# The last output chunk in written order: weights split once, the first token half normalized among the second half's products

## The chip, the cores and the metric

The kernel runs on one core of one Trainium2 chip. The metric is the device time of one launch in microseconds (us), the median of three runs. Beside the runs stands one profiled execution with its trace; rows are quoted with times from the start of its span. The engines are TensorE (PE in the rows; PEld is its weight load), VectorE (DVE), ScalarE (ACT), GpSimd (POOL) and the queue that issues most transfers (SP).

## The reference

One layer of a diffusion backbone over 512 latent tokens and 256 context tokens, model width 2048: a modulated RMSNorm, two attention mixers in parallel (differential attention and multi-head latent attention), an output projection, a second modulated RMSNorm, and a gated channel mixer of width 5632 whose gate passes a convolution of width 3 over the tokens. What matters here is its end:

```python
def _conv_ffn(h, w_up, conv_w, conv_b, w_down):
    g, u = jnp.split(h @ w_up, 2, axis=-1)
    gp = jnp.pad(g, ((0, 0), (pad, pad), (0, 0)))
    g = sum(gp[:, j:j + T] * conv_w[j] for j in range(CONV_W)) + conv_b
    return (jax.nn.silu(g) * u) @ w_down
...
x = x + g2 * _conv_ffn(h2, w_up[l], conv_w[l], conv_b[l], w_down[l])
return _rmsnorm(x, final_w)
```

The final norm divides each token by its root mean square over all 2048 features, so no output of a token can be scaled before the last of its features is known.

## The kernel before

Activations lie with features on the 128 partitions and the 512 tokens along the free axis, so one tile of 128 features is 128 x 512. Every product is made from float32 operands split in two parts: a high part cast to the matmul's format (`sc.copy` on ACT, tile `wh` or `ah`) and the rest (`ve.tensor_tensor` subtract on DVE, tile `wl` or `al`). `mm3` (L104 to L106) makes one product from three matmuls: high by high, high by low, low by high.

The channel mixer has 44 feature tiles (`ft`). From the fourth on, the up projection is a list of jobs in a manual schedule: PE, ACT, DVE and SP keep the order in which the program writes their instructions. A tile `ft` takes seven jobs `("p", ft, k)`, k from 0 to 6, of 8 + 8 matmuls (L981 with 512 columns, L983 with 256). Job i runs on PE (`run`), while `cast(i + 2)` and `low(i + 2)` split the weights two jobs ahead and `act_after` and `vec_after` handle the results of job i - 1. Two rings of three buffers load the raw weights: `ra` (tile `wr`) and `rb` (tile `rb`); `used` counts the uses of a buffer, and when it is free, `pump` issues the next load on SP. The down projection sums 11 chunks of four feature tiles; chunks 0 to 9 run as jobs `("d", c, dp)` among the up jobs, and their results are added in DRAM (`x1_d`, an accumulating transfer that POOL issues, L1002).

After job `("p", 43, 6)` four steps give the last activation: the gate is put together (L1024, L1025), scaled and convolved (`gate_in` L805, `convolve` L810 and L812), passed through SiLU (L817), multiplied (L821) and split (`ah` L823, `al` L827). The last chunk of the down projection needs it as its fourth feature tile. It stands behind the manual schedule and is ordered by the planner: `down` is called once for tokens 0 to 255 and once for tokens 256 to 511. Each call goes through 8 blocks of weights (`dp`), loads each block (L90, 512 KB), splits it whole (L80, L81), and for each of its two output tiles `dt` makes 4 products (12 matmuls of 256 columns) in a PSUM bank of its own and adds them to the residual:

```python
ve.scalar_tensor_tensor(out=x[:, ts], in0=po, scalar=modx[:, 80 + dt:81 + dt],
                        in1=x[:, ts], op0=ALU.mult, op1=ALU.add)
then(dt)
```

The first call also loads the residual tiles (L838, 16 of 256 KB). `then` squares tiles 0 to 11 (ACT, L673) and sums the squares on POOL (L674). When both calls are done, the Ln and Exp tables are loaded, and for each half `token_norm` sums over the partitions with matmuls against ones (L680, L684, the last four tiles each with a matmul of its own), makes the inverse root (`rstd`, L159 to L164), and 16 times scales a tile (DVE, L1085) and stores 128 KB (SP, L1086).

Of the kernel before, what the change touches and what calls it, by code (L numbers as in the profile page):

```python
# [17 lines left out]
P = 128  # L18
D = 2048
# [33 lines left out]
def layer_kernel(ctx: ExitStack, tc: tile.TileContext, small, rope, c_row, cc_row, x_t, ctx_t, ada, ada_k,  # L53
# [11 lines left out]
    def nm(s):  # L65
        n[0] += 1
        return f"{s}{n[0]}"
# [589 lines left out]
    ap_ = tc.alloc_tile_pool(name="ap2", bufs=32, side="right", reuse_waits="tile")  # L657
# [5 lines left out]
    for h in range(16):  # L663
        hl = a2k(F32R), a2k(F32R)
        split(hl[0], hl[1], oraw[h])
        osp.append(hl)
# [76 lines left out]
    def normed(kt):  # L743
# [4 lines left out]
        hx[kt] = (a2k(F32R), a2k(F32R) if kt >= 8 else hp.tile([P, T], F32R, tag="h12", name=nm("h12"), bufs=8))  # L748
# [7 lines left out]
    def sums(j):  # L756
# [4 lines left out]
        def put_away(t, src):  # L761
            t[j] = a2k(F32R) if t is t1 else spare.pop(0) if spare else b2k(F32R)
            split(*half(t[j]), src)
# [66 lines left out]
    def down(c, acts, ts, dst, then):  # L830

        for dp in range(8):
            wh, wl = wblock(w_dn[c, dp])
            for i in range(2):
                dt = dp * 2 + i
                x = dst[dt]
                if ts.start == 0:
                    nc.sync.dma_start(x, x1_d[dt])  # L838
                po = b_tile()[:, :ts.stop - ts.start]
                for f in range(FC):  # L840
                    o = f * 256 + i * P
                    mm3(po, (wh[:, o:o + P], wl[:, o:o + P]), [a[:, ts] for a in acts[f]], f == 0, f == FC - 1)
                ve.scalar_tensor_tensor(out=x[:, ts], in0=po, scalar=modx[:, 80 + dt:81 + dt],
                                        in1=x[:, ts], op0=ALU.mult, op1=ALU.add)
                then(dt)

# [52 lines left out]
    with tc.manual_schedule(engines={mybir.EngineType.PE, mybir.EngineType.Activation, mybir.EngineType.DVE,  # L899
# [47 lines left out]
        def cast(i):  # L947
            if i < last:
# [5 lines left out]
        def low(i):  # L954
            if i < last:
# [91 lines left out]
        for i, job in enumerate(jobs):  # L1047
            run(i)
            if job[0] == "p":
# [121 lines left out]
```

## Time and profile before

| what | us |
|---|---|
| median of the three runs | 2463.34 (2463.28 to 2465.94) |
| span of the profiled execution | 2463.1 |
| TensorE busy in it | 2379.3 (97%) |
| ends of the last up job's matmuls | about 2386.8 |
| first and last matmul of the last down chunk | 2380.61 and 2438.41 |
| first and last scaled output tile | 2443.22 and 2458.01 |

A row of the timeline gives the start, the duration (of a merged group, from its first start to its last end), engine, line, operation, output and inputs by the program's names, shapes and a count; in square brackets stands the idle time before it and what ended it. Matmuls are pipelined, so their durations overlap; the pace is read from the distance of the starts. A window row gives, for each engine, the busy time and in brackets the instructions, then the granted TensorE clock (1.00 is full speed), the mean share in which the DMA engines were busy, and GB/s. A group row gives the busy time in all and the mean duration in ns, then the idle time before.

### The profile page before, as it was taken

To read this page: it belongs to the slowest core of one execution; us is meant where nothing else is said; L and a number is where in the kernel's file an instruction comes from. 1 tells how busy PE (TensorE), PEld (TensorE's weight loads), DVE (VectorE), ACT (ScalarE), POOL (GpSimd) and SP (SyncE) were. 2 spreads that over 40 slices of the span, in tenths; PEclk is the share of its full clock that TensorE was granted. 3 is DMA by queue.
4 is the path that set the end of the run, shared out by engine and by line. 5 is a ranking of instruction groups with operands and counts; after the bars stand their busy time and mean duration, and the time that the engine had idled before them with its cause. 6 is when DMAs were issued, how large, how long until landed. Compare 5 with 4: busy or idle time off the path is not lost.

```text
span 2463.1 us, 33002 instructions
## 1 busy us (share of the span) xinstructions
PE 2379.3 (97%) x12796; PEld 1992.2 (81%) x12796; DVE 1728.2 (70%) x2274; ACT 1107.0 (45%) x1668; POOL 242.0 (10%) x266
## 2 busy tenths in 40 slices
PE   7999999999999999999999999999999999999996
PEld 3778888777677778888888888888888888888886
DVE  4668886398968777287676767676767675757576
ACT  4343121165645542254444445454545454545443
POOL 0000000121200002100101010101010101010113
PEclk8999999999999999999999999999999999999998
DMA  7868889554311158423656565656565555555564
GB/s 274 280 229 304 326 332 320 191 160 130 123 58 43 44 193 324 145 82 103 155 121 154 124 153 125 151 128 149 127 147 129 145 131 143 132 142 136 139 181 145
DMA packets 131859, 407.51 MB, mean 165 GB/s; under 512 B 14451, under 2 KB 25203, under 8 KB 123251
## 3 DMA queue, kind: packets, MB, share of 16 engines
q1 hardware_dynamic: 106422, 356.11, 43.9%
q0 software_dynamic: 25280, 49.30, 11.5%
q8 instruction: 100, 1.64, 0.3%
q14 instruction: 57, 0.47, 0.1%
HBM read 335.88 MB, written 69.48 MB: 165 GB/s over the span
## 4 chain that ended last, share of the span: by engine, by line
PE 84%; DVE 8%; ACT 3%; DMA 1%; issue 1%; POOL 1%; SPq 0%; DVEq 0%; ACTq 0%; POOLq 0%
PE y L981 11%; PE b L104 10%; PE b L105 10%; PE b L106 10%; PE z L981 6%; PE y L983 6%; PE s L104 4%; PE s L105 3%; PE s L106 3%; PE z L983 3%; PE s L482 3%; PE x L981 2%; PE pt L494 1%; PE x L983 1%; PE f L104 1%
## 5 line engine op out<-in xcount | busy, mean ns | idle before, releaser
L104 PE MATMUL b<-ah,wh 128*128 128x512 f32 (+1 forms) x768 | 287.2, 375 | 3.8 <-ACT ah L823 3.5
L105 PE MATMUL b<-al,wh 128*128 128x512 f32 (+1 forms) x768 | 287.2, 374 | 0.0
L106 PE MATMUL b<-ah,wl 128*128 128x512 f32 (+1 forms) x768 | 285.9, 373 | 0.0
L1002 POOL DMA_DIRECT2D x_d<-xs x160 | 139.7, 1007 | 1168.0 <-ACT xs L1001 1165.9
L80 ACT CAST wh<-wr 128x1024 fp32r<-128x1024 f32 (+2 forms) x134 | 132.4, 989 | 266.5 <-PE b L106 85.4
L957 DVE TENSOR_TENSOR wl<-wr,wh 128x1024 fp32r<-128x1024 f32 x125 | 152.5, 1220 | 129.2 <-ACT wh L951 129.2
L957 DVE TENSOR_TENSOR wl<-rb,wh 128x1024 fp32r<-128x1024 f32 x123 | 149.8, 1219 | 127.1 <-ACT wh L951 127.1
L81 DVE TENSOR_TENSOR wl<-wr,wh 128x1024 fp32r<-128x1024 f32 (+2 forms) x134 | 156.2, 1166 | 104.5 <-ACT wh L80 100.8
L951 ACT CAST wh<-wr 128x1024 fp32r<-128x1024 f32 x125 | 131.2, 1049 | 206.9 <-PE b L105 100.7
L951 ACT CAST wh<-rb 128x1024 fp32r<-128x1024 f32 x123 | 129.1, 1051 | 187.8 <-PE b L105 112.5
L957 DVE TENSOR_TENSOR wl<-ws,wh 128x1024 fp32r<-128x1024 f32 x123 | 150.0, 1220 | 88.9 <-ACT wh L951 88.9
L951 ACT CAST wh<-ws 128x1024 fp32r<-128x1024 f32 x123 | 128.2, 1042 | 138.3 <-DVE ws L925 52.8
L171 DVE CUSTOM_DVE_ANT_0 ada<-ada,cb,smt 128x2048 f32<-128x2048 f32 x64 | 151.1, 2363 | 54.7 <-DMA ada<-in_ada 54.6
L104 PEld LDWEIGHTS b<-ah,wh 128*128 128x128 f32 x768 | 145.8, 190 | 27.1 <-ACT ah L823 3.7
L106 PEld LDWEIGHTS b<-ah,wl 128*128 128x128 f32 x768 | 145.7, 190 | 25.6
L981 PE MATMUL y<-a2k,wh 128*128 128x512 f32 x656 | 164.0, 392 | 0.0
L105 PEld LDWEIGHTS b<-al,wh 128*128 128x128 f32 x768 | 146.1, 190 | 22.0
L104 PE MATMUL b<-a2k,wh 128*128 128x512 f32 (+1 forms) x376 | 139.8, 374 | 6.6 <-ACT a2k L751 5.0
L105 PE MATMUL b<-a2k,wh 128*128 128x512 f32 (+1 forms) x376 | 140.4, 374 | 0.4 <-DVE a2k L752 0.4
L106 PE MATMUL b<-a2k,wl 128*128 128x512 f32 (+1 forms) x376 | 139.2, 370 | 0.0
L981 PEld LDWEIGHTS y<-a2k,wh 128*128 128x128 f32 x656 | 118.6, 189 | 21.6
L981 PE MATMUL y<-b2k,wh 128*128 128x512 f32 x410 | 106.9, 391 | 0.0
(368 smaller groups left out, 5608.7 us busy)
## 6 DMA issues: line engine op xcount, KB each, us to landing
ada<-in_ada SPq DMA_DIRECT2D x64, 1024.0 KB, 6.0
rb<-in_w_up SPq DMA_DIRECT2D x123, 512.0 KB, 4.4
wr<-in_w_dn SPq DMA_DIRECT2D x96, 512.0 KB, 4.2
x_d<-xs POOLq DMA_DIRECT2D x160, 256.0 KB, 6.0
wr<-in_w_up SPq DMA_DIRECT2D x53, 512.0 KB, 4.3
wr<-in_w_f SPq DMA_DIRECT2D x34, 512.0 KB, 6.2
adak<-in_ada_k SPq DMA_DIRECT2D x32, 512.0 KB, 5.6
ada<-in_ada SPq DMA_DIRECT2D x32, 512.0 KB, 6.3
```

What stands on the lines that cost most here:

```text
L80: sc.copy(dst_h, src)
L81: ve.tensor_tensor(dst_l, src, dst_h.bitcast(F32), op=ALU.subtract)
L104: pe.matmul(out, st[0], mv[0], start=start, stop=False, **kw)
L105: pe.matmul(out, st[0], mv[1], start=False, stop=False, **kw)
L106: pe.matmul(out, st[1], mv[0], start=False, stop=stop, **kw)
L171: ve.tensor_tensor_reduce(out=junk, in0=w, in1=vec, op0=ALU.mult, op1=ALU.add, scale=1.0, scalar=col("b_ada", j), accum_out=dst[:, j:j + 1])
L482: pe.matmul(s[:, c0:c1], a, b[:, c0:c1], start=i == 0, stop=i == len(mms) - 1)
L951: sc.copy(hi, raw)
L957: ve.tensor_tensor(lo, raw, hi.bitcast(F32), op=ALU.subtract)
L981: pe.matmul(o, w[j][0], hs[j], start=start and j == 0, stop=False, skip_group_check=True)
L983: pe.matmul(o[:, h0], w[j][1], hs[j][:, h0], start=False, stop=j == 7, skip_group_check=True)
L1002: gp.dma_start(x1_d[dt], x, accum_op=ALU.add)
```

## The change

The last chunk moves into the manual schedule. Its eight weight blocks become jobs `("e", dp)` at the end of the rings: even blocks in `ra`, odd ones in `rb`. Blocks 0 and 1 are split whole by the old `cast` and `low`; blocks 2 to 7 are split in halves of 512 columns (`e_cast`, `e_low`) into buffers kept to the end, so each block is loaded and split once and serves both token halves. The residual tiles are loaded after job `("p", 43, 2)`; the pool `a2k` of 32 is parted into `a2k` and `q2k` of 16.

For the first half, PE first makes the products of feature tiles 0 to 2 of blocks 0 to 3, meanwhile ACT and DVE make the last activation with half splits of blocks 2 to 4 in between; then it makes the fourth products of these blocks, then blocks 4 to 7, then all blocks for the second half. The two output tiles of a block share one PSUM bank (`block`, `settle`). Squares are made one block late (`squares`); the sums over partitions (`root`) take three matmuls against ones. The first half's root stands on PE behind block 1 of the second half, and its 16 scaled tiles and stores (`output`, now in place) are written between the second half's blocks. At the end only the second half's root, scaling and stores are left, with stores issued by SP and ACT in turn.

```diff
@@ -654,14 +654,19 @@
 
     HT = T // 2
     tp = tc.alloc_tile_pool(name="tp", bufs=8, reuse_waits="tile")
-    ap_ = tc.alloc_tile_pool(name="ap2", bufs=32, side="right", reuse_waits="tile")
+    ap_ = tc.alloc_tile_pool(name="ap2", bufs=16, side="right", reuse_waits="tile")
+    aq_ = tc.alloc_tile_pool(name="aq2", bufs=16, side="right", reuse_waits="tile")
+
+    def q2k(dt=F32):
+        return aq_.tile([P, 512], dt, tag="q2k", name=nm("q2k"))
+
     wo = tc.alloc_tile_pool(name="wo", bufs=1, reuse_waits="tile")
     cb = wo.tile([P, D], F32, name="cb2")
     nc.sync.dma_start(cb, silu_c.to_broadcast([P, D]))
 
     osp = []
     for h in range(16):
-        hl = a2k(F32R), a2k(F32R)
+        hl = a2k(F32R), q2k(F32R)
         split(hl[0], hl[1], oraw[h])
         osp.append(hl)
 
...
@@ -827,23 +832,6 @@
         ve.tensor_tensor(hl[1], t, hl[0].bitcast(F32), op=ALU.subtract)
         return hl
 
-    def down(c, acts, ts, dst, then):
...
     acts = {}
     for ft, a in enumerate(first_pair()):
         acts[ft] = a
@@ -883,6 +871,7 @@
             if c and n_ in DOWN_AFTER:
                 jobs.append(("d", c - 1, DOWN_AFTER.index(n_)))
     last = len(jobs)
+    jobs += [("e", dp) for dp in range(8)]
 
     items_a, items_b = [], []
     for job in jobs:
@@ -890,6 +879,8 @@
             items_a.append((job, w_up[0, job[1] // 2, job[1] % 2], 1))
         elif job[0] == "d":
             items_a.append((job, w_dn[job[1], job[2]], 1))
+        elif job[0] == "e":
+            (items_a, items_b)[job[1] % 2].append((job, w_dn[NFC - 1, job[1]], 1))
         elif job[2] == 0:
             ft = job[1]
             items_a.append((("w11", ft), w_up[ft - 2, 0, 0], 2))
@@ -935,7 +926,8 @@
         def operand(job):
 
             if job[0] != "p":
-                return ra.tiles[job], lambda: ra.used(job)
+                ring = rb if job[0] == "e" and job[1] % 2 else ra
+                return ring.tiles[job], lambda: ring.used(job)
             ft, k = job[1:]
             if k == 0:
                 return ra.tiles["w11", ft], lambda: ra.used(("w11", ft))
@@ -945,14 +937,14 @@
             return rb.tiles[key], lambda: rb.used(key)
 
         def cast(i):
-            if i < last:
+            if i < last + 2:
                 raw, done = operand(jobs[i])
                 hi, lo = (wp.tile([P, 1024], F32R, tag=g, name=nm(g), bufs=3) for g in ("wh", "wl"))
                 sc.copy(hi, raw)
                 ready[i] = hi, lo, raw, done
 
         def low(i):
-            if i < last:
+            if i < last + 2:
                 hi, lo, raw, done = ready[i]
                 ve.tensor_tensor(lo, raw, hi.bitcast(F32), op=ALU.subtract)
                 if done:
@@ -1044,8 +1036,12 @@
         low(0)
         cast(1)
         low(1)
-        for i, job in enumerate(jobs):
+        for i, job in enumerate(jobs[:last]):
             run(i)
+            if job == ("p", NFT - 1, 2):
+                x1 = [a2k() for _ in range(KT)]
+                for dt in range(KT):
+                    nc.sync.dma_start(x1[dt], x1_d[dt])
             if job[0] == "p":
                 ft, k = job[1:]
                 if k in (0, 1, 2):
@@ -1059,33 +1055,140 @@
                 act_after(i - 1)
                 vec_after(i - 1)
             low(i + 2)
-        act_after(last - 1)
-        vec_after(last - 1)
-        f = live[NFT - 1]
-        silu(convolve(NFT - 1, f["g"], f["t"]))
-        acts[NFT - 1] = finish(f["t"], multiply(f["t"], f["u"]))
+        ew = {}
+        for dp in (0, 1):
+            wh, wl = ready[last + dp][:2]
+            ew[dp] = [(wh[:, c], wl[:, c]) for c in (slice(0, 512), slice(512, 1024))]
+        fresh = iter([b2k] * 16 + [lambda dt: tp.tile([P, 512], dt, tag="tp", name=nm("tp"))] * 4)
+
+        def e_cast(dp, c):
+
+            raw, done = operand(("e", dp))
+            if dp == 4:
+                if c == 0:
+                    ew[dp] = [[wp.tile([P, 1024], F32R, tag=g, name=nm(g), bufs=3) for g in ("wh", "wl")]] * 2
+                    ew[dp] = [[t[:, o:o + 512] for t in ew[dp][0]] for o in (0, 512)]
+            else:
+                ew.setdefault(dp, []).append([next(fresh)(F32R) for _ in range(2)])
+            sc.copy(ew[dp][c][0], raw[:, c * 512:(c + 1) * 512])
+
+        def e_low(dp, c):
+            raw, done = operand(("e", dp))
+            hi, lo = ew[dp][c]
+            ve.tensor_tensor(lo, raw[:, c * 512:(c + 1) * 512], hi.bitcast(F32), op=ALU.subtract)
+            if c:
+                done()
+
+        HS = (h0, h1)
+        banks = [iter([("b", 3)] * 3 + [("x", 1)] + [("y", 2), ("z", 2)] * 2),
+                 iter([("b", 3)] * 2 + [("x", 1)] + [("y", 2), ("z", 2)] * 2 + [("b", 3)])]
+        po = {}
+
+        def block(dp, th, fs):
+
+            if fs[0] == 0:
+                po[dp, th] = b_tile(*next(banks[th]))
+            t = po[dp, th]
+            for i in range(2):
+                for f in fs:
+                    o = (f % 2) * 256 + i * P
+                    mm3(t[:, HS[i]], [w[:, o:o + P] for w in ew[dp][f // 2]],
+                        [a[:, HS[th]] for a in acts[NFT - FC + f]], i == 0 and f == 0, f == FC - 1, skip=True)
+
+        def settle(dp, th):
+            for i in range(2):
+                dt = dp * 2 + i
+                x = x1[dt][:, HS[th]]
+                ve.scalar_tensor_tensor(out=x, in0=po[dp, th][:, HS[i]], scalar=modx[:, 80 + dt:81 + dt], in1=x,
+                                        op0=ALU.mult, op1=ALU.add)
+
+        ss, late = {}, {0: [], 1: []}
+
+        def squares(dp, th):
+            for i in range(2):
+                dt = dp * 2 + i
+                x = x1[dt][:, HS[th]]
+                if dt == 0:
+                    ss[th] = mm.tile([P, T], F32, tag="gu"[th], name=nm("ss"), bufs=1)[:, :HT]
+                    sc.square(ss[th], x)
+                    continue
+                q = mm.tile([P, T], F32, tag="xs", name=nm("sq"), bufs=XS)[:, :HT]
+                sc.square(q, x)
+                if dp < 7:
+                    gp.tensor_tensor(out=ss[th], in0=ss[th], in1=q, op=ALU.add)
+                else:
+                    late[th].append(q)
+
+        def root(th):
+            t = b_tile()[:, :HT]
+            for q in [ss[th]] + late[th]:
+                pe.matmul(t, ones32, q, start=q is ss[th], stop=q is late[th][-1])
+            w = mm.tile([P, 1024], F32, tag="ws", name=nm("ws"), bufs=2)
+            r = w[:, :HT]
+            rstd(r, t, D, w[:, HT:2 * HT], w[:, 2 * HT:3 * HT])
+            return r
+
+        def output(dt, th, r, queue):
+            x = x1[dt][:, HS[th]]
+            ve.scalar_tensor_tensor(out=x, in0=x, scalar=col("fw", dt), in1=r, op0=ALU.mult, op1=ALU.mult)
+            queue.dma_start(out_t[dt][:, HS[th]], x)
+
+        ft = NFT - 1
+        for c in range(2):
+            e_cast(2, c)
+            e_low(2, c)
+        v = live[ft]
+        sc.copy(v["g"][:, h1], v["y"][:, h1])
+        e_cast(3, 0)
+        ve.tensor_tensor(v["g"][:, h1], v["y"][:, h0], v["g"][:, h1], op=ALU.add)
+        e_low(3, 0)
+        t = gate_in(ft, v["g"])
+        e_cast(3, 1)
+        convolve(ft, v["g"], t)
+        silu(t)
+        e_low(3, 1)
+        e_cast(4, 0)
+        acts[ft] = multiply(t, v["u"])
+        e_low(4, 0)
+        finish(t, acts[ft])
+        e_cast(4, 1)
+        e_low(4, 1)
+        for dp in range(4):
+            block(dp, 0, range(3))
+        for dp in range(4):
+            block(dp, 0, (3,))
+            settle(dp, 0)
+            if dp in (1, 3):
+                for c in range(2):
+                    e_cast(5 + dp // 2, c)
+                    e_low(5 + dp // 2, c)
+            if dp:
+                squares(dp - 1, 0)
+        exp_ln_tables()
+        for dp in range(4, 8):
+            block(dp, 0, range(4))
+            if dp == 4:
+                for c in range(2):
+                    e_cast(7, c)
+                    e_low(7, c)
+            settle(dp, 0)
+            squares(dp - 1, 0)
+        for dp in range(8):
+            block(dp, 1, range(4))
+            settle(dp, 1)
+            squares(dp - 1 if dp else 7, 1 if dp else 0)
+            if dp == 1:
+                r = root(0)
+            elif dp > 1:
+                for dt in range(3 * dp - 6, min(3 * dp - 3, KT)):
+                    output(dt, 0, r, nc.sync)
+        squares(7, 1)
+        r = root(1)
+        for dt in range(KT):
+            output(dt, 1, r, (nc.sync, sc)[dt % 2])
     mm.release()
-
-
-    fin = tc.alloc_tile_pool(name="fin", bufs=1, side="right", reuse_waits="tile")
...
     ff.release()
+    aq_.release()
     ap_.release()
     tp.release()
     bp.release()
```

More of the change, by code (lines that the diff above doesn't have):

```diff
@@ L761, in put_away @@
         def put_away(t, src):
-            t[j] = a2k(F32R) if t is t1 else spare.pop(0) if spare else b2k(F32R)
+            t[j] = q2k(F32R) if t is t1 else spare.pop(0) if spare else b2k(F32R)
             split(*half(t[j]), src)
@@ L828, in finish @@
         return hl
-    def down(c, acts, ts, dst, then):
[L832 to L845, printed above, removed]
     acts = {}
```

19 lines of the change are left out of this document (1 added, 18 removed).

## The prediction

> **What bounds the kernel now.** I read the page first, then the chain of waits, then the timeline from 2363 us on engine by engine, then windows and groups of that stretch. A difference under 0.2% (5 us) can't be told from no change here.
>
> ```profile
> PE 2379.3 (97%) x12796; PEld 1992.2 (81%) x12796; DVE 1728.2 (70%) x2274; ACT 1107.0 (45%) x1668; POOL 242.0 (10%) x266
> PE 84%; DVE 8%; ACT 3%; DMA 1%; issue 1%; POOL 1%; SPq 0%; DVEq 0%; ACTq 0%; POOLq 0%
> ```
>
> TensorE is busy nearly all the time and holds 84% of the chain, so work saved on other engines counts only where TensorE waits for it. The stretch that the change touches is the exception. PE there:
>
> ```profile
> 2380.61 0.19 PEld L104 LDWEIGHTS b<-ah,wh 128*128 128x128 f32 x1 [0.44 <-ACT wh L80]
> 2381.19 0.63 PE L981 MATMUL z<-tp,wh 128*128 128x512 f32 x2
> 2386.78 0.28 PE L106 MATMUL b<-ah,wl 128*128 128x256 f32 x1
> 2389.42 0.28 PE L106 MATMUL b<-ah,wl 128*128 128x256 f32 x1
> 2393.24 1.01 PE L104 MATMUL b<-ah,wh 128*128 128x256 f32 x3 [3.54 <-ACT ah L823]
> 2424.73 0.28 PE L106 MATMUL b<-ah,wl 128*128 128x256 f32 x1
> 2424.85 0.28 PE L104 MATMUL b<-ah,wh 128*128 128x256 f32 x1
> 2438.41 0.28 PE L106 MATMUL b<-ah,wl 128*128 128x256 f32 x1
> ```
>
> Five matmuls of the last chunk were put ahead of the last up jobs: they cost a wait of 0.44 us and 0.58 us of their own (2380.61 to 2381.19). From 2386.78 the chunk runs alone. At 2389.4 PE runs out: three of four feature tiles are used up, and the fourth's activation (`ah`) ends its chain at 2393.2. Undisturbed starts lie 0.12 us apart. The windows show what follows the stall:
>
> ```profile
> 2390.00:2392.00 2.00, 0.00 (x0) 0.00 (x0) 1.21 (x3) 0.63 (x1) 0.00 (x0) 0.89 0.63 221
> 2392.00:2394.00 2.00, 0.76 (x3) 0.75 (x4) 1.23 (x2) 0.62 (x1) 0.00 (x0) 0.50 0.00 0
> 2398.00:2400.00 2.00, 2.00 (x17) 2.00 (x16) 1.31 (x2) 1.37 (x2) 1.12 (x2) 0.90 0.61 209
> 654.00:656.20 2.20, 0.11 (x2) 0.08 (x1) 1.88 (x4) 1.74 (x3) 1.01 (x1) 1.00 0.86 337
> 656.20:661.00 4.80, 4.41 (x15) 3.43 (x16) 3.58 (x6) 1.58 (x3) 0.00 (x0) 0.65 0.75 303
> 707.00:709.00 2.00, 0.67 (x5) 0.46 (x4) 1.77 (x4) 1.28 (x3) 0.00 (x0) 1.00 0.00 0
> 709.00:716.00 7.00, 6.90 (x42) 5.96 (x42) 5.73 (x12) 3.81 (x9) 0.00 (x0) 1.00 0.01 2
> ```
>
> The granted clock falls to 0.50 and comes back in the window from 2398. A gap of 2.1 us at 654 was also followed by a slow stretch, a gap of 1.3 us at 707 was not. So the price of this stall: 379 matmuls (the code's 2 x 16 x 4 x 3 = 384, less five) at 0.12 are 45.5 us, but PE is free only at 2438.53 (last start + 0.12), 51.75 after 2386.78: 6.3 us lost, 3.5 idle and 2.8 mostly the slow clock.
>
> After PE, the end is DVE's and SP's:
>
> ```profile
> 2438.73 0.48 DVE L843 SCALAR_TENSOR_TENSOR a2k<-b,modx,a2k 128x256 f32<-128x256 f32 x1 [0.95 <-PE b L106]
> 2438.96 1.89 PE L684 MATMUL b<-sq,ones 128*128 128x256 f32 x8
> 2440.88 0.47 ACT L159 ACTIVATE nr<-b,epst 128x256 f32<-128x256 f32 x1 [6.86 <-PE b L684]
> 2443.22 6.42 DVE L1085 SCALAR_TENSOR_TENSOR b2k<-a2k,smt,nr 128x256 f32<-128x256 f32 x16
> 2452.07 6.42 DVE L1085 SCALAR_TENSOR_TENSOR b2k<-a2k,smt,nr 128x256 f32<-128x256 f32 x16
> 2443.73 17.03 SPq L1086 DMA_DIRECT2D out_t<-b2k  x32
> 2459.87 0.90 SPq L1086 DMA_DIRECT2D out_t<-b2k  x2
> ```
>
> Two rounds of 16 scalings follow each other, and SP, at 0.53 us a store (17.03 / 32) against DVE's 0.40 (6.42 / 16), ends its last issue at 2460.77, 2.3 us behind the last scaling. The span ends 2.4 us later. From PE free (2438.5) to the end are 24.6 us.
>
> **The change part by part.** *Up jobs.* Order is now as written, so the five matmuls no longer cut in: PE is free for the chunk at 2386.78 - 0.44 - 0.58 = 2385.76.
>
> *The chunk on PE.* 384 x 0.12 = 46.1 us, if nothing stalls: 2431.84. Moving them between buffers or banks changes neither shape nor number. Whether it stalls hangs on two things, the activation and the weights. Durations for both:
>
> ```profile
> L80 ACT CAST wh<-wr 128x1024 fp32r<-128x1024 f32 x14 | 14.6, 1042 | 11.1 <-PE b L105 9.4 <-DVE wl L81 1.7
> L81 DVE TENSOR_TENSOR wl<-wr,wh 128x1024 fp32r<-128x1024 f32 x15 | 18.6, 1239 | 7.8 <-ACT wh L80 7.8
> L843 DVE SCALAR_TENSOR_TENSOR a2k<-b,modx,a2k 128x256 f32<-128x256 f32 x32 | 15.0, 480 | 8.2 <-PE b L106 7.9
> L674 POOL TENSOR_TENSOR ss<-ss,sq 128x256 f32<-128x256 f32 x22 | 23.6, 1070 | 49.3 <-ACT sq L673 48.6
> L673 ACT ACTIVATE sq<-a2k 128x256 f32<-128x256 f32 x22 | 8.6, 411 | 5.4 <-POOL ss L674 3.8 <-issue 1.4 <-DVE a2k L843 0.2
> L805 ACT ACTIVATE t<-g,smt 128x512 f32<-128x512 f32 x1 | 0.8, 815 | 1.4 <-DVE g L1025 1.4
> L812 DVE SCALAR_TENSOR_TENSOR t<-g,smt,t 128x511 f32<-128x511 f32 x1 | 0.8, 753 | 0.0
> L817 ACT ACTIVATE t<-t 128x512 f32<-128x512 f32 x1 | 0.6, 629 | 1.7 <-DVE t L812 1.7
> L823 ACT CAST ah<-t 128x512 fp32r<-128x512 f32 x1 | 0.6, 617 | 0.8 <-DVE t L821 0.8
> L827 DVE TENSOR_TENSOR al<-t,ah 128x512 fp32r<-128x512 f32 x1 | 0.7, 691 | 0.7 <-ACT ah L823 0.7
> ```
>
> PE's cover for the activation is three products of four blocks, 72 matmuls or 8.6 us: it asks for the fourth tile at 2394.4. Before it asked at 2389.5. The chain itself gets longer, because half splits (0.62 on ACT, 0.69 on DVE, as L823 and L827) stand between its steps. It starts when block 1 has landed, at L: cast 1.04 and low 1.24, two half lows of block 2 (1.4), then the gate sum 0.4 (as L843, half width), gate 0.82, convolution 1.5 (twice L812), SiLU 0.63, with a half low behind it on DVE, multiply 0.7 (as L827), `ah` 0.62; with handoffs near 0.06 that is `ah` at L + 8.8 and, behind one more half low, `al` at L + 9.6. PE takes `al` 0.12 after `ah`. So PE isn't held while L is under 2384.9, and block 1 itself is wanted (low) at 2388.0, or L under 2385.7.
>
> *When block 1 lands* is the unknown. Even blocks 0, 2 and 4 sit in `ra` and are there long before. Odd blocks are issued on SP behind the 16 residual loads:
>
> ```profile
> 2368.30 9.81 SPq L838 DMA_DIRECT2D a2k<-x_d  x16
> 2378.00:2380.00 2.00, 2.00 (x14) 1.75 (x13) 1.97 (x4) 1.31 (x3) 0.00 (x0) 1.00 1.06 409
> 2380.00:2382.00 2.00, 1.76 (x12) 1.43 (x11) 1.99 (x4) 1.04 (x2) 0.00 (x0) 1.00 0.71 272
> 2382.00:2384.00 2.00, 2.00 (x15) 1.79 (x14) 1.23 (x2) 0.72 (x1) 0.00 (x0) 1.00 0.18 24
> 2371.90 1.94 PE y L981 x8
> ```
>
> In the old run those 4.2 MB were through by about 2382 (GB/s falls to 24). A 512 KB block right behind takes 1.3 us at 409 GB/s or 1.9 at 272: L is 2383.2 to 2383.9. The other end: with 16 tiles in the pool instead of 32, every residual load must wait for up jobs 0 and 1 of the last tile to be done; if even the first waited for job 1's last matmul (2371.9, where job 2 begins) instead of 2368.3, L is 3.6 later, 2387.5. That would hold PE 1.8 us at block 1 and 0.8 more at the fourth tile. I take the early end, since the tiles that the first job frees are among the 16 and those loads can start as before; both ends go into the range. Blocks 3 and 5 follow 1.3 to 1.9 us apart, 4 and more us before PE wants them.
>
> *Later blocks.* 5, 6 and 7 are split behind the settles (L843) on DVE. From 2395 on DVE has, until block 5 is wanted at 2400.2, two settle pairs (1.9) and two half lows (1.4); block 6 (2403.1) has two more pairs and two lows before it, done near 2401.7; block 7 (2405.9) waits on ACT for squares of which only two fit until POOL adds them (1.07 each), done near 2405. The margins are 1 to 2 us. Cost nothing, covered by PE; without the cover each is a stall.
>
> *First half's root* now stands among PE's products: three sums at 0.43 us (eight passes of L684 are four sums in 1.74 between starts) are 1.3 us. Its last blocks leave PE at 2406 and 2409, so squares and adds end near 2411; PE gets there at 2414.5. Its 16 scalings (6.4 us of DVE) and stores lie under 17 us of second half products, with 16 settles (7.7): covered. PE free at 2431.84 + 1.3 = 2433.1, against 2438.5.
>
> *The tail*, from PE free, by the same rows: first settle + 0.2 and the second 0.4 behind it, done + 1.1; square + 0.07 + 0.41; one sum and its latency, 0.65; Ln to first scaling 2.34 as before (2440.88 to 2443.22): first scaling at + 4.6, last done at + 11.0. Stores alternate between SP and ACT, 0.8 us apart on each, over SP's 0.53: no backlog, so the last issue is over 0.5 us later and the span ends 2.4 after that: + 13.9. No store by ACT is in this trace; if one cost what POOL's issues do (1.0 us, L1002 on the page's group list), ACT would fall 8 x 0.2 behind, 1.6 to 2.2 us more; at best nothing differs. I take SP's cost, the nearest in kind.
>
> ```profile
> L1002 POOL DMA_DIRECT2D x_d<-xs x160 | 139.7, 1007 | 1168.0 <-ACT xs L1001 1165.9
> ```
>
> That the settles of a pair begin only when both its output tiles are done costs the 0.4 us above; if the first could go 1.4 us earlier, the tail is 0.4 shorter. The Trainium skill ("PSUM — Partial Sum Buffer", section "PSUM bank collisions raise a hardware error") says an engine must not read a bank that TensorE is writing, at whatever columns, which speaks against pairing tiles in a bank; by it the sum stays, without it it is 0.4 less. No run so far shows a shared bank.
>
> Sum: 5.4 us from PE (1.0 + 6.3 - 0.6 for the five matmuls' return - 1.3), 10.7 from the tail (24.6 - 13.9): span 2463.1 - 16.1 = 2447.0. The median lies 0.2 above the span, so **2447.2 us**.
>
> Half the splits (8 casts and 8 lows of 1.0 and 1.2 us) and 4.2 MB of loads vanish; both lay under PE, so they are worth nothing in the sum. The pool's parting holds no earlier work: all 32 tiles are free before the channel mixer begins.
>
> **The rivals.** *Block 1 late.* For it: 16 loads ahead on one queue and a smaller pool. Against: the bandwidth rows. Worked above: 2.6 us in two stalls, 2449.8; if the clock falls, 2.8 more, 2452.6. The Trainium skill ("TensorE: Matmul & The Clock Gate", Part 1) has the clock drop after an idle window of about 3.4 us; by it these stalls would leave the clock alone and 2449.8 stands. The 2.1 us gap at 654 with its 0.65 clock disagrees, so the larger figure stays possible.
>
> *The first half's output isn't hidden*, the change doing in order what it says but DVE not getting to it: root (2.3), 16 scalings (6.4) still behind PE: 2455.9. For it: DVE is strict in order and each scaling stands between settles. Against: 16 settles and 16 scalings are 14 us of DVE in 23 of PE.
>
> *Slower: the first half is paced by its splits.* One mechanism: DVE, with settles ahead of half lows, delivers blocks 4 to 7 each after PE asks, and each wait costs like the old one, 6.3 us with its clock: 25.2, so 2472.4. It decides when a split is over 2 us later than worked; at one block it costs 2453.5, at two 2459.8. Against: DVE's sum in the first half is about 20 us of 23. For: margins of 1 us at block 7.
>
> **How the numbers follow.** Forecast 0.62; block 1 late 0.15; output not hidden 0.10; paced by splits 0.13, of which one block 0.04, two 0.05, more 0.04. Faster than 2458.4 is 0.91, within 0.2% 0.05, slower 0.04. The range 2444.5 to 2456 holds the forecast with 0.4 us for the bank and 2 for rows not seen, ACT's stores, late block 1, one block and the unhidden output.
>
> **What would show it.** No idle PE over 1 us from the last up job to the end of the chunk and a granted clock of 1.00 throughout; residual loads from about 2368 on and block 1's cast near 2383; `ah` and `al` before 2394.4; 0.12 us between starts; one root among the second half's matmuls; 14 us from PE's last product to the end, stores issued by two queues. A PE wait for a cast or low of block 1 makes the first rival true, one at blocks 5 to 7 the third; scalings of the first half behind PE's end the second. A later end of the up jobs than 2386 would break the first term.

## The result and the profile after

Four runs of the changed kernel gave a median of 2451.84 us (2446.29 to 2454.10), against 2463.31 for the kernel before: a ratio of 0.9948 with a 95% interval of 0.9934 to 0.9962, so faster by half a per cent. The profiled execution has a span of 2451.9 us, at the upper end of those runs. The forecast of 2447.2 us is met within 5 us, but part of that distance is chance and part is a wrong term, and the experiments take the two apart.

The page of the changed kernel, engines and chain of waits (microseconds, share of the span):

```profile
PE 2375.5 (97%) x12788; PEld 1988.9 (81%) x12788; DVE 1726.3 (70%) x2272; ACT 1102.5 (45%) x1666; POOL 242.1 (10%) x270
PE 84%; DVE 8%; ACT 3%; DMA 3%; issue 1%; POOL 1%; SPq 0%; DVEq 0%; ACTq 0%; POOLq 0%
```

The page hardly moved; only DMA's share of the chain rose, from 1% to 3%. The timeline of PE in the last 65 us, first the chunk, then the final norm (start, duration, instruction, idle before):

```profile
2388.48 1.12 PE L975 MATMUL y<-q2k,wl 128*128 128x256 f32 x8
2389.43 0.28 PE L104 MATMUL b<-ah,wh 128*128 128x256 f32 x1
...
2418.11 0.28 PE L106 MATMUL b<-ah,wl 128*128 128x256 f32 x1
2418.23 0.59 PE L1125 MATMUL b<-ss,ones 128*128 128x256 f32 x2
2418.66 1.02 PE L1125 MATMUL b<-sq,ones 128*128 128x256 f32 x4
2419.33 0.47 PE L104 MATMUL x<-ah,b2k 128*128 128x256 f32 x1
...
2436.68 0.28 PE L106 MATMUL b<-ah,tp 128*128 128x256 f32 x1
2437.51 0.70 PE L1125 MATMUL b<-ss,ones 128*128 128x256 f32 x2 [0.56 <-POOL ss L1118]
2438.70 1.13 PE L1125 MATMUL b<-sq,ones 128*128 128x256 f32 x4 [0.49 <-ACT sq L1116]
```

No row between the first product (2389.43) and the last (2436.68) carries a wait in brackets: the chunk takes 47.37 us from the last up matmul's start to that of the last product, as 46.1 + 1.3 foresaw, and the first half's root stands inside it with 1.22 us (2418.11 to 2419.33). Windows of the chunk (length, busy of PE, weight load, DVE, ACT and POOL, granted clock, DMA share, GB/s):

```profile
2400.00:2408.00 8.00, 8.00 (x69) 8.00 (x68) 8.00 (x14) 6.02 (x12) 5.64 (x6) 1.00 0.00 0
2408.00:2416.00 8.00, 8.00 (x69) 8.00 (x68) 3.28 (x9) 3.35 (x8) 5.30 (x8) 1.00 0.01 2
2424.00:2432.00 8.00, 8.00 (x69) 8.00 (x69) 8.00 (x14) 1.92 (x5) 4.62 (x6) 1.00 0.36 123
```

PE is full at a clock of 1.00. DVE is full beside it in the first and the last of these windows, in one stretch of each half, but busy for only 3.28 of 8 us in the window between them. The other engines' timelines, for the activation, the loads and the tail:

```profile
2387.77 1.05 ACT L943 CAST wh<-rb 128x1024 fp32r<-128x1024 f32 x1 [3.19 <-DMA rb<-in_w_dn]
2395.52 0.63 ACT L828 CAST ah<-t 128x512 fp32r<-128x512 f32 x1 [0.25 <-DVE t L826]
2396.18 0.69 DVE L832 TENSOR_TENSOR al<-t,ah 128x512 fp32r<-128x512 f32 x1
2371.93 9.88 SPq L1044 DMA_DIRECT2D a2k<-x_d  x16
2400.57 2.27 DVE L1078 TENSOR_TENSOR b2k<-rb,b2k 128x512 fp32r<-128x512 f32 x2
2435.51 2.23 DVE L1133 SCALAR_TENSOR_TENSOR a2k<-a2k,smt,ws 128x256 f32<-128x256 f32 x3
2437.66 0.86 DVE L1102 SCALAR_TENSOR_TENSOR a2k<-b,modx,a2k 128x256 f32<-128x256 f32 x2
2442.20 6.42 DVE L1133 SCALAR_TENSOR_TENSOR a2k<-a2k,smt,ws 128x256 f32<-128x256 f32 x16
2443.11 5.88 ACTq L1134 DMA_DIRECT2D out_t<-a2k  x8
```

The last part of the activation (`al`) is done at 2396.87; PE asks for it 72 matmuls after 2389.43, at 2398.07. One round of 16 scalings is left behind PE, not two. From PE free (2436.80) to the end are 15.15 us, where 24.6 were before.

**Where the time went.** Two stretches compare the kernels without the stages before: from the start of the last up matmul to that of the last product, and from the moment PE is free (0.12 us after that start) to the end, called the tail. PE gains 5.40 us (before, 51.75 + 1.02 for the five early matmuls and their wait; after, 47.37), the tail 9.47 (24.62 - 15.15), together 14.87. The tail by its rows: the second round of scalings and the pause ahead of it are gone (8.85, from 2443.22 to 2452.07 before), and the last issue ends 0.37 instead of 2.28 us behind the last scaling; against that, the first scaling starts 0.7 later after PE is free, and the span ends 2.95 instead of 2.38 us after the last issue.

But the span fell by 11.2 only: the changed kernel came to its last up matmul 3.7 us late (2389.31, against 2386.66 less those 1.02). That cannot be seen in the stretch that was changed, so it was the first thing tested.

### The profile page after: what moved, and what is told of

It is laid out like the page before. It is cut to its first block, busy times and chain, and to the rows that moved or that the text cites. A ratio compares the mean times of both kernels' runs of the same rounds, so it can differ in the third digit from the quotient of the medians.

```text
span 2451.9 us, 32940 instructions
## 1 busy us (share of the span) xinstructions
PE 2375.5 (97%) x12788; PEld 1988.9 (81%) x12788; DVE 1726.3 (70%) x2272; ACT 1102.5 (45%) x1666; POOL 242.1 (10%) x270
## 3 DMA queue, kind: packets, MB, share of 16 engines
q10 hardware_dynamic: 1152, 1.05, 0.1%
## 4 chain that ended last, share of the span: by engine, by line
PE 84%; DVE 8%; ACT 3%; DMA 3%; issue 1%; POOL 1%; SPq 0%; DVEq 0%; ACTq 0%; POOLq 0%
PE y L973 12%; PE b L105 10%; PE b L104 10%; PE b L106 10%; PE z L973 6%; PE y L975 6%; PE z L975 3%; PE s L104 3%; PE s L105 3%; PE s L106 3%; PE s L482 3%; PE x L973 2%; DMA ada<-in_ada 2%; PE x L975 1%; PE f L104 1%
## 5 line engine op out<-in xcount | busy, mean ns | idle before, releaser
L104 PE MATMUL b<-ah,wh 128*128 128x512 f32 (+1 forms) x672 | 259.1, 386 | 0.0
L105 PE MATMUL b<-al,wh 128*128 128x512 f32 (+1 forms) x672 | 259.0, 385 | 0.0
L106 PE MATMUL b<-ah,wl 128*128 128x512 f32 (+1 forms) x672 | 258.0, 384 | 0.0
L80 ACT CAST wh<-wr 128x1024 fp32r<-128x1024 f32 (+3 forms) x118 | 115.9, 982 | 259.0 <-PE b L105 68.3
L81 DVE TENSOR_TENSOR wl<-wr,wh 128x1024 fp32r<-128x1024 f32 (+3 forms) x118 | 137.3, 1164 | 89.4 <-ACT wh L80 89.0
L105 PEld LDWEIGHTS b<-al,wh 128*128 128x128 f32 x672 | 126.6, 188 | 22.0
L104 PE MATMUL b<-a2k,wh 128*128 128x512 f32 (+1 forms) x352 | 133.1, 380 | 6.6 <-ACT a2k L756 5.0
L484 DVE TENSOR_REDUCE m<-s 128x1 f32<-128x768 f32 x96 | 90.5, 949 | 15.3 <-PE s L482 14.9
L993 ACT ACTIVATE xs<-b,modx 128x512 f32<-128x512 f32 x160 | 101.0, 680 | 0.5 <-PE y L973 0.3
L973 PEld LDWEIGHTS y<-b2k,wh 128*128 128x128 f32 x410 | 77.0, 188 | 17.1
```

The lines of the kernel that those rows point to most:

```text
L80: sc.copy(dst_h, src)
L81: ve.tensor_tensor(dst_l, src, dst_h.bitcast(F32), op=ALU.subtract)
L104: pe.matmul(out, st[0], mv[0], start=start, stop=False, **kw)
L105: pe.matmul(out, st[0], mv[1], start=False, stop=False, **kw)
L106: pe.matmul(out, st[1], mv[0], start=False, stop=stop, **kw)
L973: pe.matmul(o, w[j][0], hs[j], start=start and j == 0, stop=False, skip_group_check=True)
```

## The experiments

**a_again: the same kernel once more.** In the first profile of the changed kernel, PE stood still near 410 us, in a stage where both kernels issue the same work in the same order.

> The changed kernel once more, nothing edited. Theory A (the last stretch gives 14.9 us, as its trace shows between the last up tile and the end, and the 3.6 us by which it reached that stretch late are chance in the loads before 420 us): the median falls to 2448 to 2452 with runs between 2446 and 2454, and where the trace shows no long gap near 410 us the span is near 2447. Theory B (the lateness belongs to the changed program): every run is above 2450 and the trace has the gap near 410 us again.

Measured: 2447.86 us (2446.41 to 2449.98), ratio 0.9940 [0.9927, 0.9952], span 2445.7. The timeline and windows near 410 us, of the first profile and then of the second:

```profile
414.98 0.76 PE L104 MATMUL s<-wh,a2k 128*128 128x512 f32 x1 [4.58 <-DVE kl L81]
...
412.00:414.00 2.00, 0.00 (x0) 0.00 (x0) 2.00 (x4) 0.59 (x1) 0.00 (x0) 1.00 0.71 249
416.00:418.00 2.00, 2.00 (x6) 1.61 (x5) 1.85 (x3) 0.31 (x2) 0.00 (x0) 0.50 0.80 242
```

```profile
412.00:416.00 4.00, 2.98 (x14) 2.19 (x13) 1.67 (x4) 1.18 (x2) 0.00 (x0) 1.00 1.05 362
```

The gap of 4.58 us, followed by a clock of 0.50, is about 1 us with a full clock in the second. From the 2000th to the 2500th matmul of the trace (about 340 to 460 us) the first profile takes 122.3 us, the second 116.9 and the kernel before 116.4. Over ten profiles of kernels that share this order up to the last chunk, the last up matmul starts anywhere from 2381.8 to 2389.3. So the 3.7 us were chance. The two stretches, on the other hand, repeat: 47.51 and 15.07 against 47.37 and 15.15. From here on each kernel is judged by these landmarks, the time from the last up matmul's start to the end (both stretches and the 0.12 between them): 62.6 us in the first profile, 62.7 in the second. Differences are taken to the first.

**pools_only: the parting of the pool alone, on the kernel before.**

```diff
-ap_ = tc.alloc_tile_pool(name="ap2", bufs=32, ...)
+ap_ = tc.alloc_tile_pool(name="ap2", bufs=16, ...)
+aq_ = tc.alloc_tile_pool(name="aq2", bufs=16, ...)   # q2k() in place of half the a2k()
```

> The kernel before with the pool of 32 parted into two of 16 and nothing else. Theory A: 2463 as before, the last stretch as before (stall of 3.5 us, tail of 24.6 us); residual loads start at most 3.6 us later, which nothing waits for. Rival (the parting delays the channel mixer or the residuals): slower by 1 us or more between the end of the attention stage and the last up tile.

Measured: 2463.78 us, ratio 1.0003 [0.9994, 1.0012]; 75.7 us by the landmarks, before 76.5. The smaller pools hold nothing up, and all but 0.8 us at most of the gain is in the work of the last chunk.

**late_output: the first half's scalings and stores behind the second half's matmuls.** The root stays where it is.

```diff
-            elif dp > 1:
-                for dt in range(3 * dp - 6, min(3 * dp - 3, KT)):
-                    output(dt, 0, r, nc.sync)
         squares(7, 1)
+        for dt in range(KT):
+            output(dt, 0, r, nc.sync)
```

> The changed kernel with the 16 scalings and stores of the first half put behind all products, its root left where it is. Theory A (the hidden scalings are worth DVE's time in the tail): the tail from the last product to the end grows from 15.1 to about 19 us (two rounds of 16 scalings at 0.40, the first one partly under the second root), the total by 3.5 to 5. Rival (the scalings were no bound, the stores' issue or landing was): within 1 us of the changed kernel.

Measured: 2451.08 us, ratio 0.9953 [0.9940, 0.9967]; 66.2 us by the landmarks, 3.6 more, all in the tail (18.72). DVE's timeline of it, and its scalings as a group (min/median/max in ns):

```profile
2432.89 6.42 DVE L1133 SCALAR_TENSOR_TENSOR a2k<-a2k,smt,ws 128x256 f32<-128x256 f32 x16
2440.93 6.42 DVE L1133 SCALAR_TENSOR_TENSOR a2k<-a2k,smt,ws 128x256 f32<-128x256 f32 x16
L1133 DVE SCALAR_TENSOR_TENSOR a2k<-a2k,smt,ws x32: 478/480/484, 2432.9 to 2446.9; 128x256 f32<-128x256 f32 x32
```

Hiding the first half's scalings and stores is worth 3.6 us, not the 6.4 that sixteen scalings take (the other 2.3 of the second rival's 8.7 us are the root, which this run leaves among the matmuls): here the first sixteen scalings fill the wait for the second root, so only what overhangs it shows. The second thing to see is 480 ns for every scaling; in the changed kernel a group of three takes 2.23 us instead of the 1.28 that 6.42 for sixteen give.

**no_pool_sums: the second half's squares of tiles 1 to 13 and their sums left out.** This leaves part of the second half's norm undone, so that POOL adds nothing while DVE scales.

```diff
             for i in range(2):
+                if th == 1 and dp < 7:
+                    continue
```

> The changed kernel without the squares of tiles 1 to 13 of the second half and without their 13 sums on POOL (left out of the computation, so the second half's norm lacks them); PE's work and DVE's are the same. Theory A (a DVE scaling slows from 0.48 to 0.97 us where a POOL sum runs beside it): all 32 scalings at 0.48, groups of three in 1.3 instead of 2.2 us, so the last settle isn't held: tail 14.3 to 14.6 instead of 15.1, PE unchanged. Rival (in-place scaling or the running stores slow DVE): groups of three stay at 2.2.

A single run: 2446.07 us, 61.9 by the landmarks, tail 14.39. DVE's timeline with the last pair of settles, and its scalings as a group; then the same group in the changed kernel, with a sum, a scaling and a pair of squares from its timeline:

```profile
2427.68 1.27 DVE L1135 SCALAR_TENSOR_TENSOR a2k<-a2k,smt,ws 128x256 f32<-128x256 f32 x3
2429.77 0.88 DVE L1102 SCALAR_TENSOR_TENSOR a2k<-b,modx,a2k 128x256 f32<-128x256 f32 x2 [0.82 <-PE b L106]
L1135 DVE SCALAR_TENSOR_TENSOR a2k<-a2k,smt,ws x32: 474/481/485, 2416.2 to 2440.2; 128x256 f32<-128x256 f32 x32
```

```profile
L1133 DVE SCALAR_TENSOR_TENSOR a2k<-a2k,smt,ws x32: 469/480/973, 2423.7 to 2448.1; 128x256 f32<-128x256 f32 x32
2435.85 1.61 POOL L1118 TENSOR_TENSOR ss<-ss,sq 128x256 f32<-128x256 f32 x2 [1.33 <-ACT sq L1116]
2438.45 0.47 DVE L1133 SCALAR_TENSOR_TENSOR a2k<-a2k,smt,ws 128x256 f32<-128x256 f32 x1
2438.22 0.81 ACT L1116 ACTIVATE sq<-a2k 128x256 f32<-128x256 f32 x2 [2.13 <-DVE a2k L1102]
```

Without POOL's sums the group of three takes 1.27 us, none lasts longer than 485 ns, and DVE waits for PE (0.82) before the last settles, while in the changed kernel those settles wait for DVE. The edit takes the squares off ACT as well, but a square beside a scaling costs it nothing: in the changed kernel the scaling at 2438.45 has squares beside it and no sum, and takes 0.47 us, while the three from 2435.51 run beside the two sums of 2435.85. So a scaling beside a POOL sum costs up to 0.97 us instead of 0.48. The Trainium skill ("SBUF — State Buffer", section "SBUF: two separate sides") says that VectorE with two inputs in SBUF and GpSimd share a pair of ports, and that whoever starts first keeps it for the whole instruction; the rows agree, and the settles, with one input in PSUM, stay at 465 to 484 ns in the changed kernel, also in the first half, where POOL's sums run beside them.

**resplit: the weights split a second time.** Each of the second half's blocks 2 to 7 is cast and subtracted again, as the kernel before did.

```diff
             settle(dp, 1)
+            if dp < 6:
+                for c in range(2):
+                    raw = operand(("e", dp + 2))[0][:, c * 512:(c + 1) * 512]
+                    hi, lo = ew[dp + 2][c]
+                    sc.copy(hi, raw)
+                    ve.tensor_tensor(lo, raw, hi.bitcast(F32), op=ALU.subtract)
```

> The changed kernel with blocks 2 to 7 cast and subtracted once more for the second half, from the raw weights still in the buffers, into the same tiles: no load more, 12 half casts and 12 half lows more, each ahead of the first half's scalings. Theory as predicted (halving the splits is worth nothing, they lie under PE): within 0.5 us between the last up matmul and the end. Rival (DVE has no room for scalings and a second round of splits together, since a scaling beside POOL's sums takes 0.75 us and not 0.40): blocks 5 to 7 of the second half wait for their lows, 4 to 7 us more.

Measured: 2453.73 us, ratio 0.9962 [0.9949, 0.9975]; 67.6 by the landmarks, 5.0 more: 3.1 on PE, 1.9 in the tail. Its waits (engine, tile and line, who ended them; total, times, longest):

```profile
PE b L1125 <- POOL ss L1118: 2.5, 1, 2.5
PE z L106 <- DVE b2k L1184: 1.2, 2, 1.0
PE b L106 <- DVE tp L1184: 0.6, 1, 0.6
```

PE waits for the second half's lows (L1184), and the last sum waits 2.5 us for POOL, which is late because the settles are. Splits that were "worth nothing" are worth 5.0 us in this order, once the output is hidden beside them. Whether another order could hide them in the stretch where DVE has room (3.28 of 8 us busy from 2408 to 2416 in the changed kernel) was not tried.

**no_deferral: the fourth feature tile not put off.** The first four blocks run over all four tiles at once.

```diff
         for dp in range(4):
-            block(dp, 0, range(3))
-        for dp in range(4):
-            block(dp, 0, (3,))
+            block(dp, 0, range(4))
             settle(dp, 0)
```

> The changed kernel with all four products of blocks 0 to 3 made at once, so that nothing covers the last activation. Theory A (cover for the activation is what keeps PE and its clock up): PE asks for the fourth tile 1.1 us after the up jobs, waits about 5.6 us, the clock falls to 0.50 for 6.8 us: 8 to 8.5 us slower in all. Rival (only the idle counts, the clock doesn't): 5.6 us. Second rival (the weights, not the activation, come last): under 3 us.

Measured: 2458.14 us, ratio 0.9976 [0.9964, 0.9988]; 70.7 by the landmarks, 8.0 more. PE's timeline and two windows:

```profile
2394.34 0.58 PE L104 MATMUL b<-ah,wh 128*128 128x256 f32 x1 [5.20 <-ACT ah L828]
...
2394.00:2396.00 2.00, 1.52 (x5) 1.23 (x6) 1.53 (x3) 1.85 (x4) 0.00 (x0) 0.50 0.00 0
2398.00:2400.00 2.00, 2.00 (x13) 2.00 (x13) 0.88 (x2) 0.81 (x2) 0.13 (x1) 0.68 0.00 0
```

The cover of 72 matmuls is what removes the old stall: without it PE stands 5.2 us, and the clock at 0.50 and the new start cost 2.7 more on PE; the rest is in the tail.

**loads_twice: block 1 made late.** The 16 residual loads are issued twice ahead of it.

```diff
-                for dt in range(KT):
+                for dt in [*range(KT), *range(KT)]:
```

> The changed kernel with every residual tile loaded twice (16 more loads of 256 KB ahead of the odd weight blocks on SP). Block 1's cast then comes about 11 us later (4.2 MB at 370 GB/s). Theory A (block 1's landing has a slack of about 1 us, behind that PE pays one for one and the clock on top): a stall of about 9 to 10 us ahead of block 1, the clock at 0.50 for 6.8 us, 62.7 us from the last up matmul to the end become 75. Rival (weights wait is hidden by other work): under 66.

A single run: 2460.17 us; 73.3 by the landmarks, 10.7 more. ACT's and PE's timelines:

```profile
2393.90 1.04 ACT L943 CAST wh<-rb 128x1024 fp32r<-128x1024 f32 x1 [13.90 <-DMA rb<-in_w_dn]
2394.99 0.58 PE L104 MATMUL b<-ah,wh 128*128 128x256 f32 x1 [7.83 <-ACT wh L943]
```

So the first rival's mechanism is real. PE loses 11.2 us, its idle 7.8 and 3.4 for the slow clock and the new start; the tail is 0.6 shorter (14.58), since the last store here lands 1.71 us after its issue and not 2.26. In the changed kernel the cast began at 2387.77, 1.54 us before the last up matmul: in time, with little to spare.

**lows_twice: blocks 5 to 7 split slower in the first half.** Their subtractions are done twice.

```diff
-            ve.tensor_tensor(lo, raw[:, c * 512:(c + 1) * 512], ...)
+            for _ in range(2 if dp > 4 else 1):
+                ve.tensor_tensor(lo, raw[:, c * 512:(c + 1) * 512], ...)
```

> The changed kernel with each half low of blocks 5, 6 and 7 made twice (six DVE operations more, 0.68 us each alone, all in the first half). The trace of the changed kernel has block 5's last low 1.0 us, block 6's 0.4 us and block 7's 2.1 us ahead of PE's asking. Theory A (those margins are all the room there is): stalls of about 0.4 us at block 5 and 2 us at block 6, none at 7, 65 from the last up matmul to the end; the clock stays at 1.00 unless the second gap passes about 2 us. Rival (the splits have more room than the rows suggest, or DVE's order lets settles wait instead): 62.7 as before. Second rival (a slow clock follows and each later block waits): over 67.

A single run: 2449.89 us; 65.4 by the landmarks, 2.8 more. PE's rows with a wait, and the window over the first two:

```profile
2401.30 0.38 PE L106 MATMUL y<-ah,b2k 128*128 128x256 f32 x1 [1.05 <-DVE b2k L1079]
2402.63 0.39 PE L106 MATMUL y<-ah,b2k 128*128 128x256 f32 x1 [0.36 <-DVE b2k L1079]
2406.24 0.39 PE L106 MATMUL z<-ah,tp 128*128 128x256 f32 x1 [0.35 <-DVE tp L1079]
...
2399.00:2403.00 4.00, 2.59 (x20) 2.18 (x19) 3.93 (x6) 3.12 (x6) 2.63 (x3) 1.00 0.00 0
```

One more subtraction per half block, 0.7 to 1.2 us each, makes PE wait in blocks 6 and 7, not in 5 and 6 as expected: the third rival's mechanism is there too. But the clock stays at 1.00, and the three gaps cost 1.76 us and some 0.3 each for starting again, not 6.3 each.

**stores_sp: all of the second half's stores on SP.**

```diff
-            output(dt, 1, r, (nc.sync, sc)[dt % 2])
+            output(dt, 1, r, nc.sync)
```

> The changed kernel with the last 16 stores all issued by SP. Theory A (SP needs 0.5 us a store against DVE's 0.40, so two queues take a backlog away): the last issue 1.6 to 2.1 us later, the tail 16.3 to 17.2 instead of 15.1, less if a store issued by ACT lands later than one by SP. Rival (the DMA engines pace the stores): the tail as it was.

A single run: 2449.75 us; 63.9 by the landmarks, 1.3 more. Its store issues, and its last scalings:

```profile
2430.67 14.82 SPq L1134 DMA_DIRECT2D out_t<-a2k  x20
2436.85 6.42 DVE L1133 SCALAR_TENSOR_TENSOR a2k<-a2k,smt,ws 128x256 f32<-128x256 f32 x16
```

SP ends 2.2 us behind the last scaling (2445.49 against 2443.27), in the changed kernel 0.4 behind for ACT (2448.99 against 2448.62). The second queue is worth 1.3 us, less than those 1.8, since the changed kernel's last store landed 2.26 us after its issue (2448.65 to 2450.91) and this run's 1.76. That isn't ACT's doing alone: the store before it, issued by SP, took 2.46, and in loads_twice the last store, also issued by ACT, took 1.71. What makes the last stores late stays open.

**v2: what the runs point to.** The last block's two tiles get a bank each; the first half's root is one matmul over POOL's sums; its output is spread so that only one scaling stands in the group before the last settles.

```diff
-                po[dp, th] = b_tile(*next(banks[th]))
+                po[dp, th] = [b_tile(*next(banks[th]))] * 2
+                if (dp, th) == (7, 1):
+                    po[dp, th][1] = b_tile()
...
-                if dp < 7:
+                if dp < 7 or th == 0:
...
-                for dt in range(3 * dp - 6, min(3 * dp - 3, KT)):
+                for dt in (range(3 * dp - 6, 3 * dp - 3) if dp < 6 else (12,) if dp == 6 else (13, 14, 15)):
```

> The changed kernel with three small edits: the first half's squares are all summed on POOL, so its root takes one sum on PE instead of three; of its 16 scalings three move behind the last settle, so that they don't hold it; the last block's two output tiles get a bank each. Theory A: 0.86 us less on PE, 0.6 and up to 0.4 less in the tail: 61 us from the last up matmul to the end instead of 62.7; the median about 1.5 us lower, which the runs' scatter of some us hides. Rival (the moved scalings only delay the second root's DVE steps): no gain in the tail, 61.8.

Measured: 2445.73 us (2444.85 to 2446.85), ratio 0.9927 [0.9915, 0.9940]; 61.1 by the landmarks. PE's and DVE's timelines:

```profile
2427.54 0.47 DVE L1105 SCALAR_TENSOR_TENSOR a2k<-b,modx,a2k 128x256 f32<-128x256 f32 x1
2428.31 0.28 PE L106 MATMUL b<-ah,tp 128*128 128x256 f32 x1
2428.63 0.48 DVE L1105 SCALAR_TENSOR_TENSOR a2k<-b,modx,a2k 128x256 f32<-128x256 f32 x1 [0.62 <-PE b L106]
2429.07 0.70 PE L1128 MATMUL b<-ss,ones 128*128 128x256 f32 x2 [0.48 <-POOL ss L1121]
```

The first settle now runs before PE's last product instead of behind it; the root costs 0.87 us less on PE and the tail is 0.7 shorter. The first scaling comes 4.58 us after PE is free, but in no_pool_sums, with a shared bank, it was 4.69. In v2 the last sum waits 0.48 us for POOL, so what a bank of its own is worth without that wait, 0.4 us by the prediction, is not shown. This is the fastest kernel of the study, though its interval overlaps the changed kernel's, and the two were compared only through the kernel before: the 1.6 us are shown by the landmarks, not by the times.

## Why the prediction was right, and where not

*Up jobs and the chunk on PE*: right to 0.1 us. 5.4 us were forecast, 5.40 measured, and nothing stalls. Those 5.40 take the 1.02 us of the five early matmuls as given; it can be read by itself, from one up job near the end to the last:

```profile
2368.95 2.00 PE L981 MATMUL x<-a2k,wh 128*128 128x512 f32 x8
2385.83 1.11 PE L983 MATMUL y<-a2k,wl 128*128 128x256 f32 x8
```

```profile
2372.57 2.00 PE L973 MATMUL x<-a2k,wh 128*128 128x512 f32 x8
```

Before, 16.88 us lie between the two starts; in the changed kernel, from this row to 2388.48, 15.91: 0.97 less. The up jobs ended at 2389.4 and not at 2385.8 (by the prediction's last paragraph a sign against its first term), but by a_again that is chance.

*Block 1 and the activation*: right. The residual loads' first issue lies 0.64 us ahead of that row (2371.93), in the old run 0.65 (2368.30), so the smaller pool did not hold them. Moved back by the 3.6 us between the two rows, block 1's cast is at 2384.15, 0.2 behind the L of 2383.2 to 2383.9 and within the limit of 2384.9. `al` came 9.1 us after that, against 9.6. So the first rival's condition did not come about, though its mechanism is real (loads_twice).

*Later blocks*: right in outcome, but the margins lie wider apart than the "1 to 2 us" forecast. Counted as there, from the last low to a block's first matmul, they are 1.0, 0.4 and 2.1 us for blocks 5, 6 and 7 (block 5: done at 2402.84, 2400.57 + 2.27, and its first matmul 120 after the start, at 2403.83). But the last low of a block is first read by its ninth matmul, so PE's real room is 2.0, 1.4 and 3.0 us, and in lows_twice it is block 6 that waits first. Two half lows beside POOL's sums took 2.27 us here, where the prediction had 1.4.

*The tail*: the term that was mis-sized, 15.15 us for 13.9. The step "first settle + 0.2" failed: the settles began 0.98 after the last product's start (2436.68 to 2437.66), because three scalings, stretched by POOL's sums, stood ahead of them on DVE. That moved the first scaling to + 5.4, from + 4.6. Without the sums (no_pool_sums) the settles begin 0.2 after PE is free (2429.77, against 2429.45 + 0.12) and the first scaling at + 4.69, nearly as forecast. The other 0.4 us is the end: the last issue came a little sooner than forecast, but its store landed 0.5 later than the old run's last (2.26 against 1.76 us), for a reason that no run shows.

*"Half the splits … are worth nothing"* is the step that was wrong in kind, though no term of the sum hangs on it. It priced them by the cover of the kernel before, where DVE had room. The change spends much of that room on sixteen scalings, and resplit shows 5.0 us for splitting six of the eight blocks again. The sum "14 us of DVE in 23 of PE" behind the second rival's refusal was too small for the same reason: with POOL beside them the first half's scalings come 0.74 us apart (2.23 for a group of three), not 0.40, and they can't begin before the first root is there, at 2423.7; from then on DVE is full.

*The second rival's price*, 2455.9, was too high: without the root the mechanism costs 3.6 us (late_output), because the wait for the second root hides most of sixteen scalings. *The third rival's*, 6.3 us for a block, holds only for a long stall.

*Clock*: the price taken from the old stall (3.5 idle, 2.8 clock) carried over to the long gaps: beside the idle 5.2 and 7.8 us, PE lost 2.7 and 3.4. For the short ones the runs divide thus: 1.05 us in lows_twice left the clock at 1.00, as 1.3 us at 707 had in the prediction's windows, and in pools_only a gap of 1.9 us did not:

```profile
415.20:417.20 2.00, 0.13 (x1) 0.16 (x2) 0.69 (x1) 0.21 (x1) 0.00 (x0) 1.00 0.89 283
417.20:421.00 3.80, 3.80 (x11) 3.02 (x12) 0.21 (x1) 0.37 (x1) 0.00 (x0) 0.59 0.93 306
```

The prediction's doubt of the idle time of about 3.4 us that the Trainium skill ("TensorE: Matmul & The Clock Gate", Part 1) states stands: in this kernel a gap of 1.9 us is followed by a mean clock of 0.59 for 3.8 us. What decides between 1.3 and 1.9 us stays open.

The 2447.2 us, then, have a forecast gain of 16.1 us in it and a measured one of 14.9. The repeated run's 2447.86 is close to 2463.3 - 14.9 = 2448.4; the first one's 2451.84 is 3.4 us above it. Of its four runs the one with a profile had the late stage near 410 us; for the other three that isn't shown. So chance moved the first median away from the forecast, not towards it; the miss that the runs bear out is 14.9 against 16.1.

## What to carry to other kernels

Price a step that vanishes by the cover after the change, not before it: splits that were free in the old order would have cost 5 us beside the scalings of the new one. When single executions of a kernel scatter by microseconds in a stage that a change leaves alone, compare the changed stretch between two landmarks inside it. Work moved under a matmul stage should be summed per engine with what the neighbours on the same memory add to its durations, and kept from standing directly ahead of the first instruction of the tail.

## What was not expected

Three things: a scaling on DVE takes up to 0.97 us beside a sum on POOL and 0.48 without (no_pool_sums); a stage near 410 us, the same in all kernels and full of transfers, varies so much between executions that the stretch from about 340 to 460 us takes 116.0 to 122.3 us in the ten profiles, most of the 7.5 us by which their last up matmuls differ (2381.8 to 2389.3); and the last stores land 2.3 to 2.7 us after their issue in the changed kernel, 1.7 to 1.8 in loads_twice and stores_sp.

That a pair of settles in one bank begins only after both products are done was foreseen, and no_pool_sums shows it where DVE was free: it waited 0.82 us for PE and began at 2429.77, after the last product's start at 2429.45. With a bank each (v2) the first ran during the second's matmuls, before 2428.31. The Trainium skill ("PSUM — Partial Sum Buffer", section "PSUM bank collisions raise a hardware error") forbids reading a bank that TensorE is writing, and the order seen here keeps to that; what a read in between would have done no run shows.
